# Token-major grouped projections, whole-width grouped outputs and a computed TensorE order in a two-layer encoder

## The chip, the cores and the metric

The kernel runs on one core of a Trainium2 chip. The metric is the device time of one execution in microseconds (us). The engines of the core work side by side: TensorE (PE; PEld are its weight loads), VectorE (DVE), ScalarE (ACT), GpSimd (POOL), and SyncE (SP), which here only issues transfers. Transfers are also issued by ScalarE in a few places. A profile shows one execution.

## What is computed

Two layers of an encoder over 512 tokens (a grid of 8 rows by 64 columns) of width 1024, in float32, with a memory of 256 tokens:

```python
for l in range(DEPTH):                                   # 2
    x = x + hybrid_mixer(rms_norm(x, norm_mix[l]), w_in[l], ...)
    x = x + memory_cross_attention(rms_norm(x, norm_mem_q[l]), rms_norm(mem, norm_mem_kv[l]), ...)
    x = x + conv_ffn(rms_norm(x, norm_ffn[l]), w_up[l], conv_w[l], conv_b[l], w_down[l])
return rms_norm(x, norm_final)

# hybrid_mixer: proj = h @ w_in is split into na_q, na_k, na_v (8 heads of 64 each),
# g_q (8 heads), g_k and g_v (2 heads each)
g_q = apply_axial_rope(rms_norm(g_q.reshape(b, s, 8, 64), q_norm), cos, sin)
g_k = apply_axial_rope(rms_norm(g_k.reshape(b, s, 2, 64), k_norm), cos, sin)
# grouped attention: softmax(q k^T / 8) v, four q heads to each of two k/v heads, all 512 keys
# neighbourhood attention: a window of 8 x 16 grid positions with a learned bias
return concatenate([na_out, gqa_out]) @ w_out
# memory attention: 4 heads of 128; conv_ffn: silu(gate) * val with a width-3 convolution, D_FF = 2816
```

## The kernel before

**Layout.** The state is kept as eight tiles `xT` with features on the partitions and the 512 tokens on the columns. Every projection is done in three products, because a float32 operand is split in a high part and a low part (`hi`, `lo`): hi x hi, hi x lo, lo x hi (`mm3`, `gemm_T`). A product has a stationary operand of 128 x 128 and a moving one of up to 512 columns. `mm`, `sc` and `tr` are the PSUM banks (four, two, two). `r`, `t` and `s` are SBUF tiles of 1024, 512 and 16 elements per partition, in rings of 21, 14 and 24. `xg` are two large tiles: the high and the low part of the normed state, and later, when the projections are done, the transposed probabilities of the grouped heads.

**Weights.** `plan` lists all weight tiles in the order of use, mostly 1024 elements per partition. Each is loaded by SP (`raw`, two buffers), copied to its high part by ScalarE (L647) and subtracted to its low part by GpSimd (L648; VectorE for a few, letter "D" in the plan). `get_w` prepares two tiles ahead; `hi` and `lo` have four buffers each. For the last down projection six weights go to `r` tiles (letter "r") instead.

**Attention.** A layer has eight neighbourhood units (a pair of heads and two query blocks of 128), then 16 grouped units (pair `i` of the four head pairs, query block `b` of four). A unit goes through scores, softmax scaling, transposition by TensorE and the product with the values; `weave` issues these steps for successive units in slots. Between them a `Filler` puts the work that waits for nothing: projections, the first half of the output projection, memory's keys and values. `NA_FILL` and `GQA_SLOT` say how many modelled nanoseconds of products go in each slot, `N_FIRST` how many filler steps come ahead of the first unit.

Projections of q and k have features on the partitions (the weights are stationary, the tokens move, 512 columns). The neighbourhood heads' values (`project_v`, two groups `g` of 256 columns) and memory's values (`memory_values`, two groups) have tokens on the rows: the state is stationary and 256 weight columns move.

The grouped heads (`gqa_project`) are projected with features on the partitions, six groups in `GQA_ORDER`. `gqa_rope` multiplies by the rotary tables (L1255, L1256), squares on ScalarE (L1257), swaps halves by four transfers of 32 partitions, sums the squares per head with tiny products against `pairs` (followed by L1267 on VectorE and a power on GpSimd, L1272), and adds on GpSimd (L1278). For k the factor is spread over columns by four products against the identity. v is transposed back to token rows (`gqa_v`).

The grouped outputs (`gqa_values`) are computed for two query blocks at once: 256 columns, one `xg` tile for the probabilities of one such half, so the two `xg` tiles take turns. `fold` adds the two halves of the output's rows (it sums a high-part and a low-part product) and splits the result.

**Order.** The kernel's instructions are first written in program order; `Order` then reads them, simulates them with a table of durations (`Step.times`), and picks an order for ScalarE, VectorE and GpSimd (`FREE`), by due times that follow from TensorE's order. TensorE and SP keep the order as written (`InOrder`, `Counted`). The simulation is repeated `ROUNDS` = 16 times; where a product came late, what it waits for is given an earlier due time (`credit`).

**End.** `down_last` computes the last down projection (chunks 15 to 21 of the feed-forward width) in two halves of 256 tokens. For each of eight row blocks it adds to `xT` (L1704), squares (L835), sums the squares (L846) and scales by the final gain (L1674). The final norm's factor is spread over the partitions by products with the identity (`spread`, L801), multiplied in (L1682 on GpSimd, L1684 on VectorE) and stored; the first half does this beside the second half's products.

Of the kernel before, what the change touches and what calls it, by code (L numbers as in the profile page):

```python
# [1 line left out]

# [8 lines left out]
F32 = mybir.dt.float32  # L11
# [20 lines left out]
GROUPS = [(0, 8), (8, 7), (15, 7)]  # L32
EPS = 1e-6
# [6 lines left out]
NA_ORDER = [("q", 0), ("k", 0), ("q", 1), ("k", 1), ("v", 0), ("q", 2), ("k", 2), ("q", 3), ("k", 3), ("v", 1)]  # L40
# [4 lines left out]
GQA_ORDER = ["k", 0, 1, "v", 2, 3]  # L45


NA_FILL = 2430
GQA_SLOT = [3950] * 16 + [4200, 3300, 3000, 3000]
MEM_FILL = [1, 1, 2, 2, 1, 3, 1, 3, 1, 3, 1]  # L50
N_ROWS = 3
LATE = 3600
N_RAW, N_W, N_R, N_T, N_S, AHEAD, AHEAD_HELD, N_WARM, N_LATE, N_FIRST = 2, 4, 21, 14, 24, 2, 5, 7, 4, (8, 16)
# [18 lines left out]
class Counted(InOrder):  # L72
# [4 lines left out]
    def matmul(self, out, lhsT, rhs, **k):  # L77
        n = 1
        for d in rhs.shape[1:]:
            n *= d  # L80
        self.ns += max(107.0, (n + 32) / 2.4)
        return self.keep(self.engine.matmul(out, lhsT, rhs, **k))  # L82


class Free:


    def __init__(self, engine):
        self.engine = engine

    def __getattr__(self, name):
        return getattr(self.engine, name)
# [110 lines left out]
ROUNDS = 16  # L203
# [102 lines left out]
class Order:  # L306

    FREE = ("ACT", "DVE", "POOL")  # L310

    def __init__(self, tc, kept):
# [10 lines left out]
        self.credit, best = {}, None  # L323
        for _ in range(ROUNDS):
            self.due()
            end, order, late = self.run()
            if best is None or end < best[0]:
                best = end, order
            for j, by in late:
                self.credit[j] = self.credit.get(j, 0.0) + by  # L330
# [80 lines left out]
    def run(self):  # L411
# [3 lines left out]
        ready, free_at = [0.0] * n, dict.fromkeys(HAND_OVER, 0.0)  # L415
# [9 lines left out]
        order, late, product = {e: [] for e in self.FREE}, [], None  # L425
# [3 lines left out]
        def earliest(j):  # L429
# [18 lines left out]
            return max(t, free_at[steps[j].engine])  # L448

        def choose(e):  # L450

            known = [(t, j) for j in open_[e] for t in [earliest(j)] if t is not None]
# [39 lines left out]
        def over_(s, t, end):  # L492

            for q in self.after[s.index]:
                need[q] -= 1
                begun = s.engine == "PE" == steps[q].engine or (s.index, q) in self.loose
                ready[q] = max(ready[q], t if begun else end + self.wait(s, steps[q]))
                if not need[q] and steps[q].engine in self.FREE:
# [7 lines left out]
        while len(issued) < n or moving:  # L506
            best = None
            for e in HAND_OVER:
                if e in self.FREE:
                    c = choose(e)  # L510
                elif at[e] < len(written[e]):
# [16 lines left out]
            if e in self.FREE:  # L528
                open_[e].remove(j)
                order[e].append(s)  # L530
            else:
# [1281 lines left out]
```

## Time and profile before

| | before |
|---|---|
| median of 3 runs | 1351.61 us (1350.64 to 1352.07) |
| the profiled execution | 1351.96 us |
| its span in the profile | 1350.1 us |
| TensorE busy | 1337.5 us, 7018 products |
| VectorE, ScalarE, GpSimd busy | 902.1, 681.0, 698.8 us |
| moved by transfers | 139.88 MB, mean 104 GB/s |

The span runs from the first instruction to the end of the last one or the landing of the last transfer; the execution's time is 1.9 us longer. An engine's busy time is the union of its instructions' durations. TensorE's instructions overlap: one starts while the one ahead is still running, so its cost in a full stream is the distance between starts, not its duration. In a timeline row the columns are start, length of the run, engine, line, operation, what is written from what, shapes, count, and in brackets the idle time before it and what ended that. In a group's row they are count, then busy time in us and mean duration of one in ns, then the engine's idle time before the group. In a windows row they are the stretch, its length, busy time and count for PE, PEld, DVE, ACT and POOL, the granted TensorE clock, the transfers' share and GB/s.

### The profile page before, as it was taken

The numbers are of one execution on the slowest core, as the hardware profiler recorded it, in microseconds if no ns is written. First come the engines' busy times: TensorE is split into PE (matmuls) and PEld (weight loads), VectorE is DVE, ScalarE is ACT, GpSimd is POOL, SyncE is SP. The second block draws the span as 40 slices with busy tenths as digits, with TensorE's granted clock in tenths as the row PEclk, the third lists the DMA queues.
The fourth block names the chain that finished last, engine by engine and source line by source line (L and its number), as shares of the span: only waits on it lengthen the run. The fifth ranks groups of instructions, "written<-read, shape, count | busy, mean of one in ns | idle before, by whom it ended". The sixth has DMA issues, their size and how long they took to land.

```text
span 1350.1 us, 19133 instructions
## 1 busy us (share of the span) xinstructions
PE 1337.5 (99%) x7018; PEld 1146.4 (85%) x7018; DVE 902.1 (67%) x1598; ACT 681.0 (50%) x1258; POOL 698.8 (52%) x483
## 2 busy tenths in 40 slices
PE   9999999999999999999999999999999999999997
PEld 7898899888888888888898888988888888888887
DVE  6678874775984388178546678746769825862874
ACT  6776676564442244233557667855644423432441
POOL 2558766626444443443744576655554444444541
PEclk9999999999999999999999999999999999999999
DMA  7773222313333333332455531233233333333321
GB/s 217 201 190 109 79 63 73 116 45 96 96 103 98 94 94 94 109 94 82 127 155 164 140 106 49 79 95 94 63 94 98 104 94 94 93 95 109 90 83 63
DMA packets 219214, 139.88 MB, mean 104 GB/s; under 512 B 6000, under 2 KB 212080, under 8 KB 219120
## 3 DMA queue, kind: packets, MB, share of 16 engines
q1 hardware_dynamic: 218432, 138.13, 35.4%
q8 instruction: 56, 0.92, 0.3%
q10 hardware_dynamic: 688, 0.52, 0.1%
q14 instruction: 38, 0.31, 0.1%
HBM read 126.05 MB, written 2.10 MB: 95 GB/s over the span
## 4 chain that ended last, share of the span: by engine, by line
PE 93%; DVE 2%; DMA 1%; issue 1%; ACT 1%; POOL 1%; SPq 0%; DVEq 0%; POOLq 0%; ACTq 0%
PE mm L82 81%; PE sc L82 7%; PE tr L69 4%; PE tr L82 1%; DMA raw<-in_w_down 1%; POOL r L648 1%; DMA xT<-in_xT 0%; DVE t L846 0%; DMA raw<-in_w_in 0%; ACT r L1075 0%; SPq L69 0%; DVE r L875 0%; ACT hi L647 0%; ACT t L1257 0%; DVE r L1684 0%
## 5 line engine op out<-in xcount | busy, mean ns | idle before, releaser
L648 POOL TENSOR_TENSOR lo<-raw,hi 128x1024 fp32r<-128x1024 f32 (+2 forms) x268 | 511.5, 1919 | 498.6 <-ACT hi L647 494.7
L82 PE MATMUL mm<-xg,hi 128*128 128x512 f32 x1920 | 595.0, 391 | 0.0
L82 PEld LDWEIGHTS mm<-xg,hi 128*128 128x128 f32 x1920 | 356.1, 188 | 70.9
L647 ACT CAST hi<-raw 128x512 fp32r<-128x512 f32 (+2 forms) x276 | 226.3, 839 | 318.8 <-PE mm L82 267.8
L82 PE MATMUL mm<-xg,lo 128*128 128x512 f32 x960 | 373.9, 389 | 0.0
L82 PE MATMUL mm<-r,hi 128*128 128x512 f32 (+1 forms) x1096 | 316.3, 372 | 0.6 <-DVE r L1641 0.5
L1635 DVE SCALAR_TENSOR_TENSOR t<-t,par,t 128x7 f32<-128x7 f32 (+1 forms) x352 | 251.2, 773 | 25.0 <-ACT t L1628 25.0
L82 PEld LDWEIGHTS mm<-r,hi 128*128 128x128 f32 x1096 | 198.6, 189 | 35.6 <-DVE r L1641 0.7
L82 PEld LDWEIGHTS mm<-xg,lo 128*128 128x128 f32 x960 | 180.2, 188 | 37.9
L82 PE MATMUL mm<-r,lo 128*128 128x512 f32 (+1 forms) x548 | 203.6, 372 | 0.0
L82 PEld LDWEIGHTS mm<-r,lo 128*128 128x128 f32 x548 | 103.3, 188 | 17.9
L881 POOL TENSOR_SCALAR t<-t,s 128x512 f32<-128x512 f32 (+1 forms) x112 | 67.9, 622 | 75.0 <-DVE s L1323 36.1
L1620 DVE TENSOR_TENSOR t<-mm,rep 128x512 f32<-128x512 f32 x88 | 60.0, 686 | 63.0 <-PE mm L82 47.3
L1664 DVE TENSOR_TENSOR xT<-xT,mm 128x512 f32<-128x512 f32 x32 | 22.0, 686 | 104.5 <-PE mm L82 104.5
L1640 ACT CAST r<-t 128x512 fp32r<-128x512 f32 x44 | 27.3, 620 | 101.7 <-DVE t L1638 101.7
L1638 DVE TENSOR_TENSOR t<-t,t 128x512 f32<-128x512 f32 x44 | 68.2, 1551 | 4.3 <-ACT t L1637 0.5
L82 PE MATMUL sc<-r,r 128*128 128x256 f32 (+1 forms) x352 | 70.7, 333 | 0.3 <-DVE r L1081 0.3
L1628 ACT ACTIVATE t<-t,par 128x512 f32<-128x512 f32 x88 | 67.0, 806 | 1.2 <-DVE t L1620 1.2
L1317 ACT ACTIVATE t<-sc,s,qr 128x512 f32<-128x512 f32 x64 | 49.3, 775 | 32.2 <-DVE s L881 32.2
L82 PE MATMUL mm<-r,r 128*128 128x256 f32 (+1 forms) x428 | 62.5, 297 | 1.7 <-POOL r L648 1.1
L69 PE MATMUL tr<-ident,t 128*128 128x128 f32 x456 | 61.0, 273 | 0.7 <-DVE s L1267 0.7
L82 PEld LDWEIGHTS mm<-r,r 128*128 128x128 f32 x428 | 56.4, 191 | 5.0 <-POOL r L648 1.3
(160 smaller groups left out, 1607.8 us busy)
## 6 DMA issues: line engine op xcount, KB each, us to landing
raw<-in_w_up SPq DMA_DIRECT2D x88, 512.0 KB, 3.8
raw<-in_w_in SPq DMA_DIRECT2D x33, 512.0 KB, 4.1
raw<-in_w_down SPq DMA_DIRECT2D x32, 448.0 KB, 3.7
raw<-in_w_mem_kv SPq DMA_DIRECT2D x16, 512.0 KB, 3.8
raw<-in_w_down SPq DMA_DIRECT2D x16, 512.0 KB, 4.0
r<-in_bias SPq DMA_DIRECT2D x16, 384.0 KB, 4.9
r<-r SPq DMA_DIRECT2D x22, 256.0 KB, 5.6
raw<-in_w_out SPq DMA_DIRECT2D x8, 512.0 KB, 3.7
```

Source lines behind the costliest of these rows:

```text
L69: return lambda *a, **k: self.keep(op(*a, **k))
L82: return self.keep(self.engine.matmul(out, lhsT, rhs, **k))
L647: act.copy(hi[:, k], raw[:, k])
L648: (POOL if eng[0] == "P" else DVE).tensor_sub(lo[:, k], raw[:, k], f(hi)[:, k])
L881: eng.tensor_scalar(e, e, sums[:, col : col + 1], 1.0, op0=ALU.mult, op1=ALU.mult)
L1317: ACT.activation(e, sc[j], AF.Exp, bias=nmx[:, c], scale=qrs[i][:, col : col + 1], accum_out=sums[:, c])
L1620: DVE.tensor_mul(u, us[side], ffn.rep)
L1628: ACT.activation(cc, u, AF.Identity, bias=par[:, l, CB + ch : CB + ch + 1], scale=w[1])
L1635: DVE.scalar_tensor_tensor(cc[:, dst], u[:, src], wi, cc[:, dst], op0=ALU.mult, op1=ALU.add)
L1638: DVE.tensor_mul(cs[0], cs[0], cs[1])
L1640: ACT.copy(acts[j][0], cs[0])
L1664: DVE.tensor_add(xT[m], xT[m], pm)
```

## The change

1. **Grouped heads with tokens on the rows.** `wide` computes 128 tokens x 512 weight columns at a time, with four weight tiles of 2 x 512. One such unit (`project_kv`, "kv") takes the second group of neighbourhood values, grouped k and grouped v together; a second (`project_gq`, "gq") takes all eight grouped q heads. Rotary tables and gains are multiplied per token (`turn_by`), squares are summed per head by VectorE reductions, the halves are swapped by reading (`rotate`, two adds on GpSimd), and q and k are transposed by TensorE afterwards. `pairs`, the swap transfers and the transposition of v go.
2. **Memory's values** use `wide` with 512 columns; memory's keys are moved, two heads ahead of and two inside the output projection.
3. **Grouped outputs** are computed for all four query blocks: 512 columns, and the probabilities of one head pair fill both `xg` tiles.
4. **TensorE's order** is computed: `Counted` no longer keeps the written order, `product_next` picks the first product that can start, in the written order up to 240 ahead. Each of the 16 orders found is replayed twice with durations up to 4% longer and transfers starting after 1.9 to 3.1 us, and the order with the smallest sum wins.
5. **The end.** The last group is cut in chunks 15 to 18 at 512 columns and 19 to 21 in two halves; the scaling by the gain goes to ScalarE, five of eight squares go to PSUM banks, the final multiplication takes two row blocks at a time, and stores are four of 256 KB per half.
6. The fillers' sizes change, the rope table is loaded at slot 1 instead of 3, and for near k tiles one VectorE subtraction is replaced by a GpSimd copy.

```diff
-NA_ORDER = [("q", 0), ("k", 0), ("q", 1), ("k", 1), ("v", 0), ("q", 2), ("k", 2), ("q", 3), ("k", 3), ("v", 1)]
+NA_ORDER = [("q", 0), ("k", 0), ("q", 1), ("k", 1), ("v", 0), ("q", 2), ("k", 2), ("q", 3), ("k", 3), ("kv", 1), ("gq", 0)]
-NA_FILL = 2430
-GQA_SLOT = [3950] * 16 + [4200, 3300, 3000, 3000]
+NA_FILL = [[2800] * 6 + [1500] * 4, [2800] * 6 + [1400] * 4]
+GQA_SLOT = [3750] * 16 + [4200, 3300]
...
+        def product_next():
+            mine, i, seen, best = written["PE"], at["PE"], 0, None
+            while i < len(mine) and seen < AHEAD_MOST:
+                j = mine[i]
+                i += 1
+                if j in issued:
+                    continue
+                seen += 1
+                t = earliest(j)
+                if t is not None and (best is None or t < best[0] - PATIENCE):
+                    best = t, j
+                if best is not None and best[0] <= free_at["PE"] + PATIENCE:
+                    break
+            return best
...
+        def wide(key, blocks, ops, evict):
+            w, pms = [], {}
+            order = [(0, 0), (0, 1), (1, 0), (0, 2), (1, 1), (0, 3), (1, 2), (1, 3)]
+            order += [(b, i) for b in range(2, blocks) for i in range(4)]
+            for b, i in order:
+                if i == 0:
+                    pms[b] = ps_mm()
+                if i == len(w):
+                    w.append(get_w((key, i), min(AHEAD, N_W - 1 - i)))
+                bs = slice(b * P, b * P + P)
+                for k in (2 * i, 2 * i + 1):
+                    mm3(pms[b], ops[k][0][:, bs], ops[k][1][:, bs], *(v[:, k % 2] for v in w[i]), k == 0, k == KC - 1)
+                if b == blocks - 1 and i < AHEAD:
+                    prepare_w(i + 1)
+                if i == 3:
+                    evict(b, pms.pop(b))
+                yield
...
+        def turn_by(i, pm, b, xs, cc, sq):
+            n = pm.shape[1] // HD
+            for v, tab in ((xs, gtab[i][:, 1, b]), (cc, gtab[i][:, 0, b])):
+                DVE.tensor_mul(by_head(v), by_head(pm), tab.unsqueeze(1).to_broadcast([P, n, HD]))
+            ACT.activation(sq, pm, AF.Square)
+        def rotate(xs, cc):
+            xs, cc = by_head(xs), by_head(cc)
+            halves = [slice(0, HD // 2), slice(HD // 2, HD)]
+            for a, b in (halves, halves[::-1]):
+                POOL.tensor_add(cc[:, :, a], cc[:, :, a], xs[:, :, b])
...
-            ib = u % 2
-            if ib == 0:
+            i, b = divmod(u, NB)
+            if b == 0:
+                gpt[i] = []
+                for j in range(2):
+                    w = xpool.tile([P, KC, S], F32R, tag="xg", name=nm("xg"), bufs=2)
+                    gpt[i].append(w.rearrange("p (n k) (b q) -> p n k b q", n=2, q=P))
...
+            pts = gpt.pop(i)
+            po = []
+            for j in range(2):
+                po.append(ps_mm())
+                for k in range(NB):
+                    for n in range(2):
+                        PE.matmul(po[j], gvt[0][:, k, j, :], pts[j][:, n, k].rearrange("p b q -> p (b q)"),
+                                  start=k == 0 and n == 0, stop=k == NB - 1 and n == 1)
...
+            parts = [[acts.pop(j) for j in range(j0, j0 + nj)] for j0, nj in LAST]
+            for m in range(KC):
+                pm = ps_mm()
+                product(pm, 0, m, parts[0])
+                DVE.tensor_add(xT[m], xT[m], pm)
+            def finish(norm, y, last=False):
+                pr = row_bank(norm.rstd, NB // 2)
+                rep = tmp((256,))
+                ACT.copy(rep, (row_bank(norm.rstd, NB // 2) if last else pr)[:, :256])
+                for k in (0, 2, 6, 4):
+                    eng, by = (DVE, pr) if last and k < 6 else (POOL, rep)
+                    v = y[k // 4][:, k % 4 : k % 4 + 2]
+                    eng.tensor_mul(v, v, by[:, :256].unsqueeze(1).to_broadcast([P, 2, 256]))
...
+                for m in range(KC):
+                    pm = ps_mm()[:, :256]
+                    product(pm, 1, m, hops)
+                    DVE.tensor_add(xT[m][:, cs], xT[m][:, cs], pm)
+                    norms[half].square(m)
+                    ACT.activation(ys[half][m // 4][:, m % 4], xT[m][:, cs], AF.Copy, scale=gfin[:, m : m + 1])
```

More of the change, by code (lines that the diff above doesn't have):

```diff
@@ L544, in run @@
                 shared["DVE"] = t + s.busy
-            free_at[e] = t + s.busy
+            slow = 1.0 if draw is None or e not in self.FREE else 1.0 + 0.04 * draw.random()
+            free_at[e] = t + s.busy * slow
             issued.add(j)
+            while e == "PE" and at[e] < len(written[e]) and written[e][at[e]] in issued:
+                at[e] += 1
             for name in s.names:
@@ L659, in load @@
                 emit_raw()
-        while len(ready) < min(len(plan), ahead):
+        while len(ready) < min(len(plan), done[0] + ahead):
             load()
```

480 lines of the change are left out of this document (236 added, 244 removed).

## The prediction, made before the changed kernel ran

> **What bounds the kernel now.** I read the page's busy table and its chain first, then stretches of steady work, then TensorE's waits, then the end.
>
> ```profile
> span 1350.1 us, 19133 instructions
> PE 1337.5 (99%) x7018; PEld 1146.4 (85%) x7018; DVE 902.1 (67%) x1598; ACT 681.0 (50%) x1258; POOL 698.8 (52%) x483
> PE 93%; DVE 2%; DMA 1%; issue 1%; ACT 1%; POOL 1%; SPq 0%; DVEq 0%; POOLq 0%; ACTq 0%
> ```
>
> TensorE is busy for 99% of the span and is 93% of the chain that ended last. No other engine passes 67%. Time therefore follows the sum of TensorE's products plus its few holes, and a product that is removed is gained whole wherever TensorE stays fed. "Busy" does not give a product's price, because products overlap; the distance between starts does. Steady stretches of the feed-forward part give it for 512 columns, and a run of 71 products in the last stretch gives it for 256:
>
> ```profile
> 1000.00:1250.00 250.00, 250.00 (x1105) 207.01 (x1104) 159.83 (x213) 90.01 (x111) 114.26 (x48) 1.00 0.34 97
> ```
> ```profile
> 1296.14 0.40 PE L82 MATMUL mm<-r,hi 128*128 128x256 f32 x2
> ```
> ```profile
> 1300.45 4.48 PE L82 MATMUL mm<-r,r 128*128 128x256 f32 x36
> ...
> 1305.57 0.39 PE L82 MATMUL mm<-r,hi 128*128 128x256 f32 x1 [0.51 <-DVE r L1641]
> 1306.27 8.68 PE L82 MATMUL mm<-r,r 128*128 128x256 f32 x71
> 1316.06 2.54 PE L82 MATMUL mm<-r,r 128*128 128x256 f32 x19 [1.11 <-POOL r L648]
> 1323.48 0.95 PE L82 MATMUL tr<-ones,t 128*128 128x1 f32 x8
> 1324.29 5.27 PE L82 MATMUL mm<-r,r 128*128 128x256 f32 x42
> 1329.41 0.60 PE L82 MATMUL tr<-ident,s 128*128 128x128 f32 x4
> 1329.77 10.32 PE L82 MATMUL mm<-r,r 128*128 128x256 f32 x84
> 1339.92 0.50 PE L82 MATMUL tr<-ones,t 128*128 128x1 f32 x4
> ```
>
> 250 us / 1105 is 0.2262 us; with one start to spare I take 0.227 for a product of 512 columns. A single product of 256 columns lasts 0.28, so the 71 start (8.68 - 0.28) / 70 = 0.120 apart. Two products of 256 cost 0.240 where one of 512 costs 0.227: joining a pair saves 0.013. For the narrow fp32 groups:
>
> ```profile
> 52.74 1.03 PE L69 MATMUL tr<-ident,t 128*128 128x128 f32 x8
> 53.53 0.71 PE L82 MATMUL mm<-xg,hi 128*128 128x512 f32 x2
> ```
> ```profile
> 100.06 0.95 PE L82 MATMUL tr<-pairs,t 128*128 128x2 f32 x8
> 100.87 1.21 PE L82 MATMUL mm<-r,r 128*128 128x256 f32 x8
> ```
>
> Eight transposes hold the queue for 0.79, and the pair of products behind them lasts 0.71 instead of 0.62 as elsewhere, so 0.88 in all, 0.11 each. Eight of the tiny sums over `pairs` cost 0.81 and the same 0.09 behind them: 0.90.
>
> ```profile
> PE tr L82 <- POOL ident masks.py:199: 1.3, 1, 1.3
> PE mm L82 <- POOL r L648: 1.1, 1, 1.1
> PE mm L82 <- DVE r L1096: 0.7, 1, 0.7
> PE tr L69 <- DVE s L1267: 0.7, 1, 0.7
> PE mm L82 <- ACT t L1257: 0.5, 1, 0.5
> PE mm L82 <- DVE r L1641: 0.5, 1, 0.5
> PE sc L82 <- DVE r L1081: 0.3, 1, 0.3
> ```
>
> These are nearly all waits of TensorE in which nothing ran, about 5 us. That is the stock that a better order could still win.
>
> **The change, part by part, per layer.**
>
> *Products.* Before: values 1 of the neighbourhood heads are 96 products of 256 columns, and grouped k, v and four q groups 144 of 512: 96 x 0.120 + 144 x 0.227 = 44.2. After: two joint projections with tokens on the rows, 192 of 512, 43.6: -0.6. Memory's values: 96 of 256 become 48 of 512, 11.5 to 10.9: -0.6. Grouped outputs: 128 of 256 become 64 of 512, 15.4 to 14.5: -0.8.
>
> *Narrow work.* The sums of squares over `pairs` go (40 starts, five groups of eight): -4.5. The spreading of k's factor over columns goes (8 starts, priced like eight transposes): -0.9. Grouped v is no longer transposed (-4) and q and k now are (+20): 16 x 0.11 = +1.8.
>
> ```profile
> L82 PE MATMUL tr<-pairs,t 128*128 128x2 f32 x80 | 9.5, 240 | 0.0
> L82 PE MATMUL mm<-ident,t 128*128 128x128 f32 x16 | 2.2, 280 | 0.0
> L69 PE MATMUL tr<-ident,t 128*128 128x128 f32 x456 | 61.0, 273 | 0.7 <-DVE s L1267 0.7
> ```
>
> The counts (80 and 16 in two layers) agree. Sum: -5.6 per layer, **-11.3** in two.
>
> *The last down projection, once.* 336 products of 256 become 96 of 512 and 144 of 256: 40.3 to 39.1, -1.2; the last norm adds four narrow starts to the first half, +0.45. The 43.8 us from 1296.14 to 1339.92 also hold two holes. The 36 products from 1300.45 end their starts at 1304.65 and the next comes at 1305.57: 0.8 too late, for the last activation. The 71 end at 1314.67 and the next comes at 1316.06: 1.3 too late, for a weight's low part. After, the first 22 us use chunks 15 to 18, so chunk 21's activation has time; a 256-column weight tile lasts 24 x 0.227 = 5.4 us where one lasted 21 x 0.120 = 2.5. Both holes should go: -2.1; I take **-1.9**, and 0 as the other bound. Then 9 x 0.120 = 1.1 us per row block remain for VectorE (two adds) and ScalarE (square and scaling), at 0.42 each by these rows: 0.84 of 1.1, just fed, so no gain beyond that.
>
> ```profile
> L1704 DVE TENSOR_TENSOR xT<-xT,mm 128x256 f32<-128x256 f32 x16 | 6.6, 419 | 8.9 <-PE mm L82 8.9
> L835 ACT ACTIVATE t<-xT 128x256 f32<-128x256 f32 x16 | 6.6, 418 | 23.4 <-DVE xT L1704 21.3 <-DVE s L863 2.1
> ```
>
> *Tail.*
>
> ```profile
> 1343.56 0.37 ACT L801 COPY rep<-tr 128x256 f32<-128x256 f32 x1 [2.51 <-PE tr L82]
> 1343.97 2.08 DVE L1684 TENSOR_TENSOR r<-xT,tr 128x256 f32<-128x256 f32 x6 [2.06 <-ACT rep L801]
> ```
>
> VectorE waited 0.4 for ScalarE's copy of the same bank. The copy now reads a second bank, and three double multiplications at 0.685 last as long as six. Against it stand larger last transfers and GpSimd's four double multiplications for the first half, up to 4 x 1.43 = 5.7 in the final 5 us; the last power waits behind them if the order is bad. -0.4 to +1.5; I take 0.
>
> *Other engines.* VectorE and ScalarE come out within about 1 us per layer (fewer, wider folds and evictions against head-wise sums). GpSimd gains work:
>
> ```profile
> L1278 POOL TENSOR_TENSOR t<-t,t 128x512 f32<-128x512 f32 x10 | 14.3, 1428 | 0.0
> L648 POOL TENSOR_TENSOR lo<-raw,hi 128x512 fp32r<-128x512 f32 x122 | 157.6, 1313 | 85.3 <-ACT hi L647 81.5 <-PE sc L82 2.9 <-PE tr L69 0.8
> L894 POOL TENSOR_TENSOR r<-t,r 128x256 fp32r<-128x256 f32 x14 | 10.3, 739 | 4.8 <-ACT r L893 4.7
> ```
> ```profile
> 100.00:125.00 25.00, 25.00 (x150) 21.98 (x150) 20.25 (x44) 18.52 (x47) 20.24 (x20) 1.00 0.40 109
> 125.00:150.00 25.00, 25.00 (x134) 21.30 (x133) 22.11 (x41) 14.92 (x32) 20.53 (x16) 1.00 0.36 106
> ```
>
> It loses five rotations at 1.43, 7.2 (and a copy, left out); it gets ten half-wide adds at 0.74, k's scaling and two table products at 1.43, and two weight halves from VectorE at 1.31: 14.3. That is +7.1 us per layer, in a stage where GpSimd is already at 20.5 of 25 us. The work starts earlier (filler before the first scores grows from 8 and 16 steps to 12 and 24), so I price it at nothing while TensorE has other products; without that cover it is 7.1 per layer. ```profile
> 50.00:75.00 25.00, 25.00 (x147) 21.95 (x146) 17.48 (x43) 19.40 (x47) 14.67 (x18) 1.00 0.92 252
> ```
>
> On SP's queue the twenty swap transfers of the rotation per layer go. The rope table halves to 256 KB and is issued two slots earlier, with the gains behind it, into layer 0's stretch where the transfers are at 0.92: at 252 GB/s it delays what is queued behind it, weights and bias, by 1 us. A weight tile feeds 5.4 us and two are split ahead, so I price it at nothing; without that cover, +1.
>
> *TensorE's order.* It is no longer as written, but computed: the next product that can start within 60 ns, up to 240 ahead. Two of the holes above belong to steps that vanish (the sums at L1267, the squares at L1257): -1.2 visible. The early ones (L1096, L1081) may be filled: -0.5. New holes are the unknown: the planner's durations are estimates, and TensorE now follows them too. Bounds: -3 (all waits of the middle gone) and +8 (GpSimd's 7.1 in one layer and SP's 1). I take -1.2 - 0.5 + 1.0 = **-0.7**, near the row of waits, since written order already left so little.
>
> Sum: -11.3 - 1.2 + 0.45 - 1.9 + 0 - 0.7 = -14.65. The profiled execution itself took 1351.96 us (span 1350.1 and 1.9 around it), 0.35 above the median 1351.61; from the median I get 1351.6 - 14.6 = **1337.0**.
>
> [...]
>
> **Rivals.**
> 1. *The order fills nearly everything* (no new holes, all waits of the middle and a clean tail): 1351.6 - 12.05 - 2.1 - 3 - 0.4 = 1334, down to 1331. For it: the search replays its orders with disturbed durations. Against: the start, where the first hole is the identity's building.
> 2. *GpSimd or model errors hold TensorE back*: work falls by 12.05, the last stretch by 1.9, but the middle gains 7.1 in one layer: 1345. For it: 20.5 of 25 us. Against: the weights are split ahead.
> 3. *Joining saves nothing* (the fixed part per product is not paid twice): only the narrow work counts, 2 x (-4.5 - 0.9 + 1.8) + 0.45 - 1.9 - 0.7 = -9.4: 1342. Against: two clean rows.
> 4. *Slower, through the buffers of the probabilities.* One head group's transposed probabilities now fill both large buffers that two half groups shared, so the next group's first eviction must wait until all 16 output products (3.6 us) are done.
>
> ```profile
> L874 ACT CAST xg<-tr 128x512 fp32r<-128x512 f32 x20 | 10.7, 591 | 1.0 <-PE tr L69 0.9
> ```
> ```profile
> L875 DVE TENSOR_TENSOR xg<-tr,xg 128x512 fp32r<-128x512 f32 x64 | 43.4, 685 | 9.9 <-ACT xg L874 9.4
> ```
>
> A unit's two evictions are 2 x (0.59 + 0.685) = 2.55 us; if TensorE has nothing else at each of four hand-overs per layer, that is 8 x 2.55 = 20.4, 1357. It decides from 1.8 us per hand-over on, and only if the filler has run out; behind the waiting evictions stand VectorE's score maxima. Against: out-projection and memory products are there to be moved in.
> 5. *The order is in effect the written one*: the middle keeps its holes, 1338.
>
> **How the numbers follow.** Forecast with rival 5 (1333 to 1341): 0.62. Rival 1 below that: 0.12. Rivals 2 and 3 (1341 to 1348): 0.20. Rival 4: 0.05, some of it near the old time. 0.2% (2.7 us) is about what a measurement can tell from no change. Faster 0.93, same 0.03, slower 0.04. The range 1331 to 1345 leaves out about two in ten.
>
> **What would show it.** The joined projections at 0.227 per start and no rows on `pairs`; the last stretch without waits on L648's counterpart; a list of TensorE's waits no longer than now. Wrong it would be if TensorE waited for evictions into the large buffers, or for GpSimd's rotations or powers, for more than some 10 us together, or if the end after the last product grew by over 2 us.

## The result, and the profile after

The changed kernel takes 1341.82 us (median of 4 runs, 1341.38 to 1344.25), beside 1351.34 us (1350.64 to 1352.07) for the kernel before. The ratio is 0.9934, with a 95% interval of 0.9920 to 0.9947: 9.5 us faster. The forecast was 1337.0 (1331 to 1345): the sign and the range are right, the gain was put 4.8 us too high.

The profiled execution of after is the one at 1344.25, 2.4 us above the median. Where that matters I use the profile of the same kernel taken again (a0_again, 1342.38), and say so.

The page of after, span, busy table and chain:

```profile
span 1342.5 us, 18121 instructions
PE 1330.8 (99%) x6544; PEld 1117.7 (83%) x6544; DVE 886.5 (66%) x1574; ACT 683.4 (51%) x1258; POOL 706.1 (53%) x496
PE 91%; DVE 3%; ACT 3%; issue 1%; DMA 1%; POOL 0%; SPq 0%; POOLq 0%; ACTq 0%; DVEq 0%
```

TensorE has 474 products less, VectorE is busy for 15.6 us less, and GpSimd, for which the prediction had 7.1 us more in each layer, for 7.3 us more in the whole span. The bound is still TensorE. But its share of the chain fell from 93% to 91%, and that of DVE and ACT together rose from 3% to 6%.

After, groups of TensorE by shape (count, busy us and mean ns, idle time before), and one steady stretch of the feed-forward part:

```profile
L95 PE MATMUL mm<-hi,xg 128*128 128x512 f32 x256 | 87.5, 397 | 0.5 <-DVE r L1152 0.5
L95 PE MATMUL mm<-xg,r 128*128 128x512 f32 x128 | 30.4, 390 | 0.0
L1366 PE MATMUL tr<-ident,t 128*128 128x128 f32 x40 | 6.4, 278 | 0.0
```
```profile
1000.00:1250.00 250.00, 250.00 (x1104) 207.01 (x1103) 158.19 (x208) 89.52 (x111) 113.01 (x48) 1.00 0.33 97
```

The first row holds the joined projections' products with the weights' high part. The outputs of the grouped heads (second row) are 128 products of 512 where 256 of 256 stood, q and k are transposed in 40 pieces, nothing reads `pairs`, and a product of 512 columns still costs 250 / 1104 = 0.226 us.

To see where the time went I took, over all starts of TensorE in the trace, the distance to the next start, less the usual distance of that shape (0.2267 us for 512 columns, 0.120 for 256, 0.1095 for a transpose, 0.112 for narrower ones). The usual distances add up to "products"; what is left over is a hole, put down to the stage where it lies. So the row of products is a count times fixed distances. That the distances hold is seen where TensorE is fed all the time: from 300 to 650 and from 1000 to 1275 us the holes of each kernel add up to less than 0.1 us. The first 1.34 us before any product are the same in all kernels to 0.01 us.

| us | before | after | after, profiled again | forecast of the difference | found (again - before) |
| --- | --- | --- | --- | --- | --- |
| products | 1327.70 | 1315.64 | 1315.64 | -12.05 | -12.06 |
| holes, 0 to 50 us | 4.72 | 3.57 | 3.30 | -0.5 | -1.42 |
| holes, layer 0's attention (50 to 300) | 2.47 | 4.79 | 4.99 | with layer 1: -0.2 | +2.52 |
| holes, layer 1's attention (650 to 1000) | 4.11 | 9.50 | 7.77 | | +3.66 |
| holes, 1275 to the last start | 2.84 | 1.52 | 1.41 | -1.9 | -1.43 |
| last start to the end | 6.93 | 6.10 | 6.14 | 0 | -0.79 |
| span | 1350.1 | 1342.5 | 1340.6 | -14.65 | -9.5 |

The work fell as forecast; since the distances are those that the forecast used, the agreement to 0.01 us tests its counts and not the distances. The two attention stages did not come out as forecast: their holes grew by 6.2 us where it had -0.2 (-1.2 for steps that vanish, +1.0 for new ones).

After, TensorE's waits in which nothing ran (us in total, times, longest):

```profile
PE mm L95 <- DVE t L1322: 2.6, 1, 2.6
PE tr L95 <- POOL ident masks.py:199: 1.3, 1, 1.3
PE tr L1296 <- DVE r L1169: 1.0, 2, 0.8
PE mm L95 <- DVE r L1152: 0.5, 1, 0.5
PE tr L95 <- POOL s L944: 0.2, 1, 0.2
```

These are 5.6 us, about as much as before (5.1 us in the rows of the prediction). In this execution all of the middle's end with VectorE; before, one ended with ScalarE. The account by starts is longer than this list, since a hole of some tenths inside a run of products is no wait in it. After, VectorE's and GpSimd's rows of the timeline around the largest one, and the product that was late (start, length of the run, engine, line, what, and in brackets the idle time and what ended it):

```profile
793.65 3.88 DVE L1001 SCALAR_TENSOR_TENSOR r<-r,par,r 128x256 fp32r<-128x256 f32 x1
794.57 1.45 POOL L1361 TENSOR_TENSOR t<-t,t 128x256 f32<-128x256 f32 x2
795.96 1.29 POOL L978 TENSOR_TENSOR r<-t,r 128x512 fp32r<-128x512 f32 x1
797.33 2.56 POOL L714 TENSOR_TENSOR lo<-raw,hi 128x512 fp32r<-128x512 f32 x2
797.57 0.42 DVE L1321 TENSOR_TENSOR t<-mm,t 64x256 f32<-64x256 f32 x1
798.02 0.67 DVE L1399 TENSOR_SCALAR s<-s,geps 128x8 f32<-128x8 f32 x1
798.72 0.42 DVE L1322 TENSOR_TENSOR t<-mm,t 64x256 f32<-64x256 f32 x1
799.28 0.77 PE L95 MATMUL mm<-hi,r 128*128 128x512 f32 x1 [2.57 <-DVE t L1322]
```

One VectorE instruction of memory's preparation (L1001), which has a median of 0.48 us, lasts 3.88 us, across GpSimd's L1361, L1361 and L978, which follow one another without a gap, and ends at 797.53, 0.2 us after GpSimd has gone on to L714. Behind it on VectorE stand L1321, L1399 and the fold L1322, and behind the fold TensorE, for 2.57 us. That GpSimd holds the instruction is so far a reading of these rows; experiments below bear on it. A second loss follows the pause; after, a stretch of the windows view (stretch, length, busy us and count of PE, PEld, DVE, ACT and POOL, granted clock, transfers):

```profile
799.00:802.40 3.40, 3.12 (x8) 2.46 (x9) 3.34 (x10) 0.66 (x1) 0.90 (x1) 0.51 0.39 117
```

For 3.4 us, from 799.05 on, TensorE's clock is granted at half. The eight products there, seven of 512 columns and a transpose, take 3.3 us from start to start where the usual distances give 1.7.

After, at the end, the waits behind the weights' low part and the last activation are gone from the list (the holes there fell by 1.4), and the final multiplications on VectorE wait for TensorE, no longer for ScalarE's copy:

```profile
1328.39 5.05 POOL L1786 TENSOR_TENSOR r<-r,t 128x512 f32<-128x512 f32 x4 [2.21 <-ACT t L1782]
...
1335.97 1.88 DVE L1786 TENSOR_TENSOR r<-r,tr 128x512 f32<-128x512 f32 x3 [1.99 <-PE tr L95]
```

GpSimd's four double multiplications for the first half end at 1333.4, before GpSimd's last power starts at 1334.1, and that power waited for VectorE's sum. So the mishap that the prediction feared there, the power standing behind them, didn't come.

### The profile page after: what moved, and what is told of

Same layout as the page of the kernel before. It is cut to its first block, busy times and chain, and to the rows that moved or that the text cites. A ratio compares the mean times of both kernels' runs of the same rounds, so it can differ in the third digit from the quotient of the medians.

```text
span 1342.5 us, 18121 instructions
## 1 busy us (share of the span) xinstructions
PE 1330.8 (99%) x6544; PEld 1117.7 (83%) x6544; DVE 886.5 (66%) x1574; ACT 683.4 (51%) x1258; POOL 706.1 (53%) x496
## 4 chain that ended last, share of the span: by engine, by line
PE 91%; DVE 3%; ACT 3%; issue 1%; DMA 1%; POOL 0%; SPq 0%; POOLq 0%; ACTq 0%; DVEq 0%
PE mm L95 80%; PE sc L95 7%; PE tr L1451 2%; PE tr L95 1%; PE tr L1296 1%; DVE r L952 1%; ACT hi L713 1%; DMA r<-in_bias 0%; DMA raw<-in_w_in 0%; ACT t L1274 0%; ACT r L1167 0%; PE tr L1630 0%; DVE r L1169 0%; ACT r L1148 0%; DVE r L1001 0%
## 5 line engine op out<-in xcount | busy, mean ns | idle before, releaser
L714 POOL TENSOR_TENSOR lo<-raw,hi 128x512 fp32r<-128x512 f32 (+3 forms) x278 | 528.1, 1909 | 524.6 <-ACT hi L713 519.4
L95 PE MATMUL mm<-xg,hi 128*128 128x512 f32 x1728 | 533.5, 390 | 0.0
L713 ACT CAST hi<-raw 128x512 fp32r<-128x512 f32 (+3 forms) x282 | 232.5, 842 | 335.3 <-PE mm L95 282.6
L95 PEld LDWEIGHTS mm<-xg,hi 128*128 128x128 f32 x1728 | 322.5, 188 | 65.7
L95 PE MATMUL mm<-r,hi 128*128 128x512 f32 (+1 forms) x1200 | 346.6, 371 | 0.0
L95 PE MATMUL mm<-xg,lo 128*128 128x512 f32 x864 | 336.3, 389 | 0.0
L95 PEld LDWEIGHTS mm<-r,hi 128*128 128x128 f32 x1200 | 218.4, 188 | 39.4 <-DVE r L952 1.0
L95 PE MATMUL mm<-hi,xg 128*128 128x512 f32 (+1 forms) x384 | 111.1, 359 | 0.5 <-DVE r L1152 0.5
L95 PEld LDWEIGHTS mm<-hi,xg 128*128 128x128 f32 x384 | 68.3, 189 | 9.8 <-DVE r L1152 0.9
L95 PE MATMUL mm<-lo,xg 128*128 128x512 f32 (+1 forms) x192 | 68.7, 358 | 0.0
```

The costliest lines, as they stand in the source:

```text
L95: return self.engine.matmul(out, lhsT, rhs, **k)
L713: act.copy(hi[:, k], raw[:, k])
L714: (POOL if eng[0] == "P" else DVE).tensor_sub(lo[:, k], raw[:, k], f(hi)[:, k])
```

## Experiments

Times are medians with the lowest and highest run; ratios are against the kernel before, run beside them on the same chip (1350.88, 1351.45 and 1351.67 us on the three chips used). The first four runs, after profiled again among them, are from one chip; where a run from another is set against after, up to 0.8 us may be the chip's.

### The same kernel again

> The changed kernel once more, unaltered, for a profile of an execution near its median (the first one lay 2.4 us above it) and a second interval. Theory P (the hole of 2.6 us at 796 us, behind a VectorE subtraction of 3.88 us, is a chance of that execution): the hole is gone or under 1 us, no half-clock stretch follows it, and the span is 1340 +/- 1. Rival O (the hole is what the computed order leaves there every time): the subtraction lasts over 2 us again and TensorE waits over 2 us at the same place. Both expect a ratio to the kernel before of 0.992 to 0.995.

1342.08 us (1341.68 to 1342.89), ratio 0.9936 (0.9919 to 0.9953). The 3.88-us instruction and the half clock in the middle are not there: L1001's longest is 1.60 us, and the longest wait of TensorE is another:

```profile
PE tr L1451 <- DVE r L1169: 1.4, 1, 1.4
```

Layer 1's attention still has 7.8 us of holes. So the large pause and the half clock behind it explain most of the profiled execution's 2.4 us above the median (it has 9.5 us of holes there) and not the missing gain.

### The computed order: undone, and alone

```diff
-class Counted(Free):
+class Counted(InOrder):
...
-        return self.engine.matmul(out, lhsT, rhs, **k)
+        return self.keep(self.engine.matmul(out, lhsT, rhs, **k))
```

> The changed kernel with TensorE kept in its written order, all else computed as in the changed kernel. If the holes that ate part of the gain come from TensorE following modelled times (rival O), the time falls below the changed kernel's 1341.8, to about 1337, which was the forecast with the holes of before. If the written order has only become worse fed (fewer, larger pieces, both large buffers used at once), the computed order pays: 1345 or more. If the order is in effect the written one, 1341.8 +/- 1.

1359.55 us (1358.69 to 1361.39), ratio 1.0067 (1.0052 to 1.0082). The products are the same 1315.64 us; the holes are 34.8 us, about 11.5 of them from 100 to 225 and 15.2 from 775 to 900. Written order, TensorE's waits:

```profile
PE tr L72 <- DVE s L958: 7.7, 6, 1.3
PE tr L72 <- DVE r L1169: 4.8, 2, 3.7
PE tr L72 <- DVE xg L952: 2.1, 5, 0.5
```

The other half is the old kernel's products with the new planner:

> The kernel before with the changed planner alone (computed order for TensorE, replays with disturbed durations), no product changed. By the forecast's own step the order is worth -0.7 us without new holes' allowance changed (bounds -3 and +8): 1350.6, with 7018 TensorE instructions as before. If the order itself costs what the change fell short by, 1351.3 + 5 = 1356. If it removes the holes of the middle: 1346 to 1348.

1351.09 us (1350.48 to 1352.92), ratio 1.0004 (0.9995 to 1.0013). On the old products the computed order is worth nothing that can be measured; on the new ones it is worth 17.5 us. Without it the change would be 8.7 us slower than before (with fillers and slots as the change sets them, which may suit the computed order). So the two parts can't be priced one by one and added. The three rows of waits above all end with VectorE; that its work now comes in lumps, and that the order's gain is to get out of their way, fits them but wasn't tested.

In the trace of the computed order alone the holes of the two attention stages are 7.1 us, before 6.6. So it is not the computed order as such that brings the 6.2 us of the changed kernel.

### Grouped outputs two blocks at a time again

```diff
-            i, b = divmod(u, NB)
-            if b == 0:
-                gpt[i] = []
...
+            ib = u % 2
+            if ib == 0:
...
+                        PE.matmul(po[:, j], gvt[0][:, k, j, :], pts[j][n][:, k].rearrange("p i n -> p (i n)"),
```

> The changed kernel with grouped outputs again for two query blocks at a time: 128 products of 256 columns per layer instead of 64 of 512, and the two large buffers taking turns again. The products alone cost 2 x 64 x 0.013 = +1.7 us. If the full-width outputs cost nothing in waiting: 1343.5. If the hand-over of both large buffers between head pairs is what ate the gain (rival 4 at a small price, 6 hand-overs of about 0.8 us), the holes go and the time falls to 1338 or 1339.

1342.97 us (1342.93 to 1343.99), ratio 0.9944 (0.9929 to 0.9959): 0.9 more than the changed kernel beside it. The edit also brings back folds of half the width, which the lines above don't show. The products alone are 1.70 us more (128 x 0.0133 by the rows), so 0.8 us is left that the full-width outputs might cost in waiting, less than the 2 us that the last run shows to be chance. The rival with 20 us of hand-overs is refuted.

### The tiny sums put back

```diff
+            pv = ps_t()
+            for c in range(NB):
+                PE.matmul(pv[:, 2 * c : 2 * c + 2], sq[:, c * P : (c + 1) * P], pairs, start=True, stop=True)
```

Their results are read by nobody.

> The changed kernel with the tiny sums of squares put back beside the new way: five groups of eight narrow starts per layer against the old 128 x 2 matrix, their results read by nobody. By the forecast's price (0.90 us a group) 10 groups cost +9.0: 1351. If TensorE's holes swallow them, less: under +5. If narrow starts between joined products cost more than the row of before showed, over +11.

1351.71 us (1350.31 to 1354.06, 10 runs), ratio 1.0004 (0.9995 to 1.0013), 9.6 more than after profiled again. In the trace, nine of the ten groups of eight cost 0.84 to 0.93 us each over the usual distances of the products around them, counted from the product ahead to the third one behind; the tenth has a wait in it. The trace also has a half-clock stretch of 3.4 us, from 803.5.

```profile
L95 PE MATMUL tr<-pairs,t 128*128 128x2 f32 x80 | 9.5, 241 | 0.0
```

Eighty products with two columns each are worth some 0.11 us apiece, 9 us together: by themselves about as much as the whole change won.

### The joined products split again

```diff
-                    mm3(pms[b], ops[k][0][:, bs], ops[k][1][:, bs], *(v[:, k % 2] for v in w[i]), k == 0, k == KC - 1)
+                    for n, (x, y) in enumerate(((ah, bh), (ah, bl), (al, bh))):
+                        for h in (0, 256):
+                            PE.matmul(pms[b][:, h : h + 256], x, y[:, h : h + 256], start=(k, n, h) == (0, 0, 0),
+                                      stop=(k, n, h) == (KC - 1, 2, 256))
```

The same is done to the grouped outputs and the last down projection, 704 pairs in all. That is more than the change joined, since grouped k, v and four q groups had 512 columns before.

> The changed kernel with every joined product issued as two of 256 columns (the three projections with tokens on the rows, the grouped outputs and the first part of the last down projection): 304 per layer and 96 at the end, 704 products doubled, all else as it was. By the rows (0.240 against 0.227) +9.4 us: 1351. [...] Holes elsewhere may change this by 1 or 2 us.

1355.13 us (1353.28 to 1356.42, 10 runs), ratio 1.0026 (1.0017 to 1.0036), 13 more than after. In its trace the 2196 distances from one product of 256 columns to another have a median of 0.120 us, the figure from the rows of before, so 704 doubled products are worth 704 x 0.0133 = 9.4 us. Another 3.9 are holes, among them a half-clock stretch of 3.4 us from 815.8.

```profile
L95 PE MATMUL mm<-hi,xg 128*128 128x256 f32 x640 | 114.4, 285 | 0.1
```

Rival 3, joining saves nothing, is refuted: a pair costs 13.3 ns more than the product that it replaces (two at 0.120 against one at 0.2267).

### Memory's preparation earlier in layer 1

```diff
-            if s >= 5:
+            if s >= 2 + 3 * (l == 0):
```

Seven of layer 1's instructions L1001 fall into the 40 us at the change from neighbourhood to grouped units, where before had two of them (there L925). In the groups of that stretch, before, and then after profiled again:

```profile
L925 DVE SCALAR_TENSOR_TENSOR r<-r,par,r 128x256 fp32r<-128x256 f32 x2 | 1.6, 803 | 0.0
```
```profile
L1001 DVE SCALAR_TENSOR_TENSOR r<-r,par,r 128x256 fp32r<-128x256 f32 x7 | 5.7, 832 | 0.1
```

The same stretch in the windows view, before and then after profiled again:

```profile
775.00:815.00 40.00, 39.49 (x215) 33.63 (x216) 30.28 (x59) 25.66 (x53) 31.27 (x25) 1.00 0.41 113
```
```profile
775.00:815.00 40.00, 37.24 (x196) 29.36 (x195) 37.63 (x80) 31.21 (x73) 30.10 (x32) 1.00 0.21 66
```

VectorE went from 30.3 to 37.6 of 40 us, with 80 instructions for 59, and TensorE, which it feeds, from 39.5 to 37.2. (The changed kernel is some us ahead by then, so the two windows don't hold quite the same work; from 790 to 830, before, VectorE is at 31.9.) But fullness alone doesn't make the holes. In layer 0 of the same execution, after profiled again, VectorE is nearly as full and TensorE hardly loses:

```profile
115.00:155.00 40.00, 39.78 (x213) 32.74 (x212) 37.12 (x82) 33.95 (x77) 30.89 (x33) 1.00 0.24 70
```

Summed without regard to overlap, VectorE's rows give the 41 us of the expectation.

> The changed kernel with the preparation of memory's operands three slots earlier in layer 1 (the transfer and eight pairs of ScalarE copies and VectorE subtractions). Theory V: the holes between 775 and 825 us come from VectorE, which is busy 41 of 40 us by its rows from 775 to 815 and has seven of these subtractions (5.7 us) there; with them gone from there the holes of layer 1's attention shrink from about 6 us to 3 and the time falls to 1339 or 1340. Rival W (the holes are what the computed order misjudges, wherever the work lies): 1342 +/- 1.

1344.32 us (1343.93 to 1346.28), ratio 0.9951 (0.9936 to 0.9966): 2.4 slower than after, not faster. Memory earlier, the timeline:

```profile
795.87 1.46 POOL L1361 TENSOR_TENSOR t<-t,t 128x256 f32<-128x256 f32 x2
796.19 0.42 DVE L1322 TENSOR_TENSOR t<-mm,t 64x256 f32<-64x256 f32 x1
796.64 4.45 DVE L1399 TENSOR_SCALAR s<-s,geps 128x8 f32<-128x8 f32 x1
797.26 1.31 POOL L978 TENSOR_TENSOR r<-t,r 128x512 fp32r<-128x512 f32 x1
798.52 2.54 POOL L714 TENSOR_TENSOR lo<-raw,hi 128x512 fp32r<-128x512 f32 x2
801.01 0.41 DVE L1321 TENSOR_TENSOR t<-mm,t 64x256 f32<-64x256 f32 x1
```

Now another VectorE instruction is held across GpSimd's run, one with eight elements per partition and a median of 0.25 us: it adds the epsilon to a head's sum of squares. It lasts 4.45 us, until GpSimd's fourth instruction in a row ends (from the second L1361 on). What stands behind it on VectorE is late, TensorE waits, and for 6.8 us the clock is granted at half. The list of waits and the windows view:

```profile
PE sc L95 <- ACT t L1429: 3.0, 2, 2.6
```
```profile
804.80:811.60 6.80, 6.31 (x14) 4.46 (x15) 4.43 (x10) 5.61 (x14) 5.14 (x5) 0.50 0.21 70
```

So it was not L1001 as such, and neither the 1339 to 1340 of theory V nor the 1342 of its rival came true. A new theory, argued from these two cases (3.88 and 4.45 us, both with their operands in SBUF): any VectorE instruction with its operands in SBUF can be held while GpSimd has no gap, and what costs is how many such instructions fall into GpSimd's full stretch.

### Head sums left out

```diff
-                DVE.tensor_reduce(ss, by_head(sq), axis=AX.X, op=ALU.add)
+                DVE.tensor_reduce(ss, by_head(sq)[:, :, 0:1], axis=AX.X, op=ALU.add)
```

> The changed kernel with the squares of a grouped query head summed over one element of 64 only, so 63 of 64 are left out: four VectorE reductions per layer of 0.67 us become short. Theory V: VectorE is relieved by 2.2 us per layer just where it is full, and the time falls by 1.5 to 3, more than half of it around 100 to 130 and 780 to 825 us. Rival W: no change beyond 1 us.

1339.52 us (1338.98 to 1340.85), ratio 0.9911 (0.9894 to 0.9928): 2.3 to 2.6 less than after. Holes from 775 to 925 fall from 6.24 (after, profiled again) to 4.66; layer 0's stay (4.66 for 4.63 from 50 to 275). That is in favour of VectorE being too full at the change-over of layer 1. How far a time of this size can be trusted, the last run shows.

### The epsilon on ScalarE; with memory earlier; with GpSimd's gaps in the planner

```diff
-                DVE.tensor_scalar(v, ss, geps[:, 1, b : b + 1], 1.0, op0=ALU.add, op1=ALU.mult)
+                ACT.activation(v, ss, AF.Identity, bias=geps[:, 1, b : b + 1], scale=1.0)
```

> The changed kernel with one small step moved: the addition of the epsilon to a query head's sum of squares (128 x 8, four per layer) goes from VectorE, where it took 0.2 to 4.45 us in the traces so far, to ScalarE (about 0.25 us). Theory P2 (VectorE's instructions that read only SBUF are held for as long as GpSimd's instructions follow each other without a gap, and TensorE's larger holes come from that): holes at 795 to 810 us shrink below 1.5 us, no half-clock stretch, time 1338.5 to 1340.5. Theory V alone (VectorE has simply too much to do there): 0.7 us less work of VectorE's changes little, 1341 to 1342.

1339.60 us (1338.72 to 1340.18), ratio 0.9912 (0.9897 to 0.9927). Holes from 775 to 925 are 3.16 (6.24), no stretch in the middle runs at half clock, and the moved step takes 0.30 us on ScalarE. The same windows row:

```profile
775.00:815.00 40.00, 38.96 (x211) 32.37 (x211) 36.40 (x81) 33.77 (x80) 33.37 (x35) 1.00 0.26 80
```

TensorE is busy for 39.0 of the 40 us instead of 37.2, with VectorE hardly less full (36.4 for 37.6). With this in place, memory's preparation can move:

> The same step on ScalarE, and the preparation of memory's operands three slots earlier in layer 1, as in the run that came out at 1344.3 with that step held for 4.45 us. Theory P2 with V: with nothing to be held there the move now pays, 1337 to 1339. If moving memory's preparation is bad in itself: 1343 to 1344 again.

1338.57 us (1338.24 to 1340.33), ratio 0.9908 (0.9893 to 0.9923). This beats both kernels: 13.1 us below before, 3.3 below after. The edit that by itself came with 2.4 us more now comes with none; the instruction that was held there is no longer on VectorE. Its page, waits and the same windows row:

```profile
span 1336.4 us, 18115 instructions
PE 1327.4 (99%) x6544; PEld 1115.9 (83%) x6544; DVE 881.0 (66%) x1566; ACT 686.8 (51%) x1266; POOL 707.5 (53%) x496
```
```profile
PE tr L95 <- POOL ident masks.py:199: 1.3, 1, 1.3
PE mm L95 <- POOL lo L714: 0.5, 1, 0.5
PE tr L95 <- POOL s L944: 0.2, 1, 0.2
```
```profile
775.00:815.00 40.00, 39.82 (x215) 32.35 (x214) 33.63 (x74) 32.69 (x76) 32.91 (x34) 1.00 0.25 77
```

VectorE is at 33.6, TensorE at 39.8, as full as before the change, and no wait on VectorE over 0.2 us is left. Last, the planner was told that a VectorE instruction reading two wide operands from SBUF starts only in a gap of GpSimd; the port that the expectation names is an assumption of the planner, shown by no run:

```diff
+            if j in self.two and shared["POOL"] > t:
+                t = shared["POOL"] + 40.0
```

> The same step on ScalarE, and in the planner a VectorE instruction with two operands in SBUF now waits until GpSimd's queue has a gap of 40 ns, instead of until GpSimd's running instruction ends. P2: the planned order avoids such waits, the remaining holes of attention fall by 1 to 2 us against the run with the step alone. If the planner's present picture of the port is good enough: within 1 us of that run.

1340.65 us (1340.22 to 1341.36), ratio 0.9922 (0.9906 to 0.9939): no gain over the epsilon alone. Much of the holding did go. The page of the epsilon on ScalarE, and then of the same with GpSimd's gaps in the planner:

```profile
PE 1327.6 (99%) x6544; PEld 1116.0 (83%) x6544; DVE 879.8 (66%) x1566; ACT 686.2 (51%) x1266; POOL 707.5 (53%) x496
```
```profile
PE 1327.5 (99%) x6544; PEld 1115.8 (83%) x6544; DVE 871.3 (65%) x1566; ACT 686.1 (51%) x1266; POOL 700.4 (52%) x496
```

The same instructions take 8.5 us less on VectorE and 7.1 less on GpSimd, so that time was waiting inside them and not work. (Memory's longest instruction is 0.94 us here and was 0.98 with the epsilon alone, 1.60 in after profiled again.) But TensorE's holes are 14.9 us for 14.2: by this account the waiting moved from inside the instruction to in front of it.

### How much the plan's draw is worth

```diff
-ROUNDS, REPLAYS, MARGIN, SHARES, STRETCH, SEED = 16, 2, 100.0, (0.0, 0.0, 0.5, 1.0, 2.0), 250, 0
+ROUNDS, REPLAYS, MARGIN, SHARES, STRETCH, SEED = 16, 2, 100.0, (0.0, 0.0, 0.5, 1.0, 2.0), 250, 1
```

> The changed kernel with another seed of the planner's random draws and nothing else. It says how much of a difference between two plans is chance: if the time is within 1 us of 1341.9, differences of 2 us between the runs above have causes; if it moves by 2 us or more, they may be the draw's, and only what the traces show of single holes stands.

1340.12 us (1339.85 to 1340.59), ratio 0.9917 (0.9902 to 0.9932). Another seed of the planner's search, nothing else, is worth 1.7 to 2.0 us. So every edit that draws a new order comes with an error that no number of runs makes smaller, some 2 us by this one draw. The gains of the head sums and of the epsilon alone and the losses with memory earlier and with GpSimd's gaps in the planner are of that size; their times prove nothing, and only the holes in the traces can speak for them. From 775 to 925 us these are 5.8 us with the other seed and 6.1 with the outputs in halves, close to the 6.2 of after profiled again, though the orders differ. The 3.2 us with the epsilon on ScalarE, and 2.8 with memory earlier as well, stand clear of that. The written order (17.5), the tiny sums (9.6) and the split pairs (13) stand far outside. The best kernel's 3.3 lies beyond this one draw, but one draw is no distribution, and its interval (to 0.9923) touches that of after profiled again (from 0.9919): that it beats before is shown, that it beats after by its edits is likely.

## Why the prediction was right, and where it failed

**What bounds, and the price of products: right.** The sum of the work, -12.05, came out at -12.06 with the counts of the trace and the same prices. The two prices under it were tested by themselves: a tiny sum 0.11 us (0.84 to 0.93 for a group of eight), a joined pair 13 ns (0.120 between products of 256 columns again in the split kernel).

**The last stretch: right in kind.** Forecast -1.9, found -1.43. **The tail**, put at 0 with -0.4 as the best case, gained 0.79, more than its bound: the copy from a second bank took ScalarE out of VectorE's path, as described, but the three double multiplications also ended sooner (1.88 us for 2.08). **The start** gained 1.42 where the early holes were put at 0.5.

**The failed step is the term for TensorE's order**, "-1.2 - 0.5 + 1.0 = -0.7". The 1.0 for new holes in the two attention stages was the wrong size: net of the vanished steps they grew by 6.2 us, not -0.2. It was taken near the row of waits of before, "since written order already left so little". But the written order is as good as the computed one only with the old products (1351.09 computed, 1350.88 written); with the new ones it is 17.5 us slower. The row of waits measured a balance that the change itself removed. The reason given for new holes, that the planner's durations are estimates, doesn't carry them either: with the old products the computed order adds 0.5 us to the holes of attention. About 2 of the 6.2 us belong to the draw, since with the other seed these holes are 10.9 us instead of 12.8.

**Beneath it lies the sentence on the other engines**, that VectorE comes out "within about 1 us per layer". Over the span it is better than that (902.1 to 886.5). The mean hid the place: at the change-over in layer 1, where the holes from 775 to 925 us grew from 1.5 to 6.2, VectorE went from 30.3 to 37.6 of 40 us, with the folds of the last neighbourhood units, the head-wise sums and seven of memory's scalings together, and the chain's share of DVE and ACT rose from 3% to 6%. That a full VectorE alone isn't the cause is seen in layer 0 (37.1 of 40, TensorE 39.8); which of its instructions stands ahead of TensorE's operand, and how long it is held, counts as well. The prediction priced GpSimd's 7.1 us there at nothing and looked at VectorE only in sum.

**Rivals.** The second, GpSimd or the planner's errors hold TensorE back (1345), came nearest by its mechanism: in the two places shown, after and with memory earlier, a stretch of GpSimd holds TensorE back, but through VectorE, whose instruction lasts 3.88 and 4.45 us meanwhile, and not through late weights. The third had the time almost to the digit (1342) by accident: the gain that it denied was there, and the holes took about as much. The split pairs refute it. Rival 1 is refuted by the holes, 4 by the outputs in halves, 5 by the written order at 1359.55.

**What stays open.** Layer 0's holes from 50 to 275 are 4.3 us or more in every version of the new products but the other seed's (3.7); no run went at them. How often the long holding comes in runs that aren't profiled isn't known. And whether the full VectorE or the holding by GpSimd costs more in layer 1 wasn't separated: each edit changed both, and the draw's 2 us lies over it. So the place of layer 1's holes is shown, and that taking VectorE's work away there can shrink them; their cause in detail is in part argued.

## What to carry to other kernels

Price each product by the distance between starts, one row per shape: that part of the forecast held here, and narrow products weren't cheap (0.11 us for two columns of float32). Then look at the engine that feeds TensorE in windows of some 40 us at every place where the change moves work, not in the sum over the span: an engine at 66% on average was at 94% where the holes were. A full window is a place to look, not yet a cause: another at 93% cost next to nothing. Where an order is searched for, run a second seed before believing 2 us.

## What the runs showed of the hardware

Beside several GpSimd instructions that follow one another without a gap, a VectorE instruction lasted far longer than its like: 3.88 us for one with a median of 0.48 (after), 4.45 us for one with a median of 0.25 and only eight elements per partition (memory earlier). With such instructions planned into gaps of GpSimd, the same 1566 instructions of VectorE took 8.5 us less (879.8 to 871.3), and the same 496 of GpSimd 7.1 less (707.5 to 700.4). That agrees with GpSimd holding them; by what, and why the one in after stood over three GpSimd instructions and not over the first alone, wasn't tested.

A pause of TensorE of 2.57 us was followed by 3.4 us with the clock at half, one of 2.64 us (memory earlier) by 6.8 us, one of 1.4 us (after, profiled again) by none. But the length of the pause alone doesn't tell which. With the tiny sums back the pause ahead of the half clock was 1.74 us, with the split pairs there were two of 0.90 and 1.14 us, the clock falling within the second; and in the written order the longest of all, 3.67 us from 791.87 on, was followed by full clock. In the clock records of after the changes at 799.05, 802.47 and 1334.95 come 791.89, 3.41 and 532.48 us after the one before (the first counted from the record's start, at 7.16): 232, 1 and 156 times 3.4133. In before the only change, at 1346.31, comes 1341.44 us after the record's start: 393 times. (The one at 1334.95 and that of before lie at the kernel's end.) By such steps the stretch ahead of the fall in after, and the two across which the written order's pause lies, are these in the windows view:

```profile
795.64:799.05 3.41, 1.07 (x5) 0.56 (x3) 3.31 (x4) 2.09 (x5) 3.33 (x4) 1.00 0.45 154
```
```profile
790.27:793.68 3.41, 1.60 (x12) 1.18 (x10) 3.34 (x11) 2.71 (x9) 0.41 (x1) 1.00 0.00 0
793.68:797.09 3.41, 1.55 (x9) 1.41 (x10) 3.03 (x7) 3.29 (x9) 1.71 (x4) 1.00 0.01 2
```

Ahead of the falls in after, with memory earlier, with the tiny sums back and with the split pairs, TensorE was busy for 1.07, 1.13, 1.67 and 1.70 us of such a stretch. The 1.60 and 1.55 us of the written order brought none, so TensorE's busy time in that stretch doesn't tell which either. What brings the fall stays open.
